# A one-core block kernel with attention, a recurrence and routed experts: router one-hots, bias table and last adds moved to other places in the order

## The chip, the core and the metric

The kernel runs on one core of one Trainium2 chip. The metric is the device time of one execution in microseconds (us). A core has five engines with queues of their own: TensorE (PE, whose weight loads are shown as PEld), VectorE (DVE), ScalarE (ACT), GpSimd (POOL) and SyncE (SP, which here only issues transfers). Each works through its instructions in the order in which they were put into its queue.

## What is computed

A sequence of 512 tokens with 1024 features goes through one block:

```python
proj = x @ w_in
o_a = dilated band attention of 3 groups x 4 heads, with a learned bias per distance bucket
o_b = a gated recurrence of 8 heads (forget gate f, running sums of log f)
o_c = attention of 4 heads over a memory of 256 rows
merged = sum of gate_i * (o_i @ w_branch_i)
x = layer_norm(ALPHA * x + merged @ w_out)                    # ln1
eid, weights = two experts of the best of 4 groups, for each token
y = sum over a token's two experts of weight * ((silu(x @ w_gate) * (x @ w_up)) @ w_down)
x = layer_norm(ALPHA * x + y)                                 # ln2
```

All of it is float32. There are 32 experts, and their weights (100 MB) are read once.

## The kernel before, in words

The tokens stand in four tiles of 128 rows, called c = 0 to 3. A float32 product of the first part is made of three matmuls of rounded parts (high by high, high by low, low by high); `split` (L82 to L84) makes the parts, the high one by a cast on ACT (L83), the low one by a subtraction on DVE (L84). The order of the instructions on each engine is made by a scheduler from the program's order and the dependences; it may pull an instruction ahead of others if its operands and its buffers are free. Inside `tc.manual_schedule(engines=...)` the named engines keep the order of the source.

**Start** (L148 to L166). Ten matmuls of a zeroed tile on itself run while the first rows are loaded. Then eight pieces of x arrive, each is split, and the first product `acc0` (a forget gate of the recurrence) is accumulated piece by piece.

**Forget gates** (L241 to L268). `forget(hd)` makes a product, a Sigmoid on ACT and a linear map on DVE for each of eight heads. `log_sums(hd)` takes the Ln on ACT and a running sum on DVE. Sigmoid and Ln need different activation tables, so that table loads stand between them (L244, L249).

**Memory attention** (L271 to L307), in the pool `c`, and then two gates `sgc` of it, whose tiles have the tag `sg` in the pool `gate` (three buffers).

**Bias table** (L311 to L334), in a pool `a0` of its own, opened when `c` is closed. The table of 32 buckets by 12 heads is loaded and split (L313 to L320); then for five pieces of 512 columns (the last has 256) GpSimd loads the bucket one-hots into `bk` (L327), ACT casts them into `bkr` (L329), PE multiplies (L331), ACT copies the result into `rows` (L333), and GpSimd stores them into DRAM, `bias_d` (L334). `bias_copies(h)` (L336 to L339) later spreads them over rows of `rep_d`, with three transfers per head.

**Recurrence** (L343 to L499), in a pool `b` that is opened after `a0` is closed. GpSimd clears `batt` and `bq` (L485, L487), `hgrn_front` makes the products of a head and copies one of them into `bw` on ACT (L352), and `hgrn_back` does the rest.

**Band attention, merge and first norm.** `residual` (L757) adds x and takes statistics; `norm_and_route(c)` (L707) normalises tile c, transposes it, multiplies by the router's weights, finds the two experts of each token on DVE (L721 to L734), counts the tokens of each expert before this one with PE (L739), and lets `picked(c, 0, oh0)` (L700, L743) make the one-hots of the first pair of experts: for each row of a pair's 128 slots the token that it takes. `gain_and_store(c)` (L745) multiplies by the gain and adds the offset, on GpSimd for tiles 0 to 2 and on DVE for tile 3, and stores the rows for the later gathers.

**Experts** (L1084 on). The 32 experts are treated as 16 pairs. `gather(p)` (L803) brings a pair's tokens: for p = 0 and 1 (`PEG = 2`) PE multiplies the four tiles of x1 with one-hots (L814, 8 matmuls per tile, each seen as two records); the one-hots of pair 1 are made by `picked` inside `gather(1)` (L811), on DVE. Later pairs are fetched from DRAM by an indirect transfer (L799). `gate_up(p)` (L829) multiplies by the first two weight matrices, `down` (L1048) by the third. The weights come through a ring of 33 buffers of 512 KB (`ring`, L658), in the order of use, issued by SP; a buffer is loaded again when the matmuls of its expert are done with it. In the loop p = 0 makes `gate_up(0)`, `tables` and `overflow_tables` (the slots, tokens and weights of all pairs, mostly small DVE instructions) and then `gather(1)`.

**End** (L1172 to L1225). DVE and PE are in source order. Each of the four tiles gets x1, the outputs of pairs 0 to 13 read back from DRAM (`back[c]`, two parts that `both(c)`, L1180, adds up on DVE) and the outputs of the last two pairs, added up in PSUM by `begin` and `finish`; `norm_out` (L1139) takes statistics on DVE (L1143), scales and stores. Tiles 0 to 2 use ACT (L1158) and GpSimd (L1159) for the last steps, tile 3 DVE alone (L1156). `both(2)`, `both(3)` and the addition of `back[3]` to tile 3 of x1 (L1216 to L1220) stand on DVE between the norms of the tiles.

Of the kernel before, what the change touches and what calls it, by code (L numbers as in the profile page):

```python
# [10 lines left out]
F32 = mybir.dt.float32  # L11
# [21 lines left out]
PEG = 2  # L33
# [3 lines left out]
def build(tc, ins, out, dbg=None):  # L37
# [117 lines left out]
    with tc.tile_pool(name="xs", bufs=2, side="right") as xsp:  # L155
        for k in range(8):
# [8 lines left out]
            for n, (wt, m) in enumerate(((w0[0], xh), (w0[0], xl), (w0[1], xh))):  # L165
                TE.matmul(acc0, wt[:, ks], m[:, k, :], start=k == 0 and n == 0, stop=k == 7 and n == 2)  # L166

# [102 lines left out]

    och = T(op_, [128, 4, 512], F32R, tag="oh4")  # L271
# [37 lines left out]


    with tc.tile_pool(name="a0", bufs=2, side="right") as tp:  # L311
        tab = T(tp, [97, 12], tag="tab")
        V.memset(tab, 0.0)  # L313
        for r0 in (0, 64):
            V.memset(tab[r0:r0 + 33, :], NEG)
            G.dma_start(tab[r0:r0 + 32, :], ins["rel_bias"])
        tabr, tabh = (T(tp, [97, 12], F32R, tag=t) for t in ("tabr", "tabh"))
        S.copy(tabr[0:64, :], tab[0:64, :])
        S.copy(tabh, tab)
        V.tensor_tensor(tabr[64:97, :], tab[64:97, :], tabh[64:97, :].bitcast(F32), op=OP.subtract)  # L320
        for j in range(5):
            w = min(512, 2304 - j * 512)
            js = slice(j * 512, j * 512 + w)
            bk = T(tp, [97, 512], tag="bk")
            V.memset(bk[32:64, :w], 0.0)
            for r0 in (0, 64):
                G.dma_start(bk[r0:r0 + 33, :w], ins["bucket"][:, js])  # L327
            bkr = T(tp, [97, 512], F32R, tag="bkr")
            S.copy(bkr[:, :w], bk[:, :w])  # L329
            pt = bank("sc")  # L330
            TE.matmul(pt[:12, :w], tabr, bkr[:, :w], start=True, stop=True)  # L331
            rows = T(tp, [12, 512], tag="rows")
            S.copy(rows[:, :w], pt[:12, :w])  # L333
            G.dma_start(bias_d[:, js], rows[:, :w])  # L334
# [361 lines left out]
    oh0 = T(lp, [128, 4, 128], tag="oh0")  # L696
# [3 lines left out]
    def picked(c, p, to):  # L700

        for e in range(2):
            m = 2 * p + e
            V.tensor_scalar(to[:, c, e * 64:(e + 1) * 64], i64, cums[:, c, m:m + 1], memb[:, c, m:m + 1],
                            op0=OP.is_equal, op1=OP.mult)

    def norm_and_route(c):  # L707

        r = x1[:, c, :]
        mu, sd = scales(lp, stats[:, c])  # L710
        xT = T(lnp, [128, 8, 128], tag="x1T")
# [614 lines left out]
```

## Time and profile before

| what | value |
|---|---|
| median of 3 runs | 1138.49 us (1136.7 to 1140.42) |
| the profiled execution, its own time | 1141.1 us |
| its span, first to last instruction | 1138.7 us |
| mean granted TensorE clock | 0.993 of full |
| busy: PE, DVE, ACT, POOL | 96%, 43%, 39%, 7% |
| bytes moved by DMA | 201 MB, 177 GB/s on average |

The span is the time between the first and the last instruction in the trace; the own time of the execution holds a little more, 2.4 us here. A row of a timeline gives start, duration, engine, line, operation and tiles, and in brackets how long the engine was idle before it and what ended that. Busy times of PE are of pipelined matmuls whose ends are modelled.

### The profile page before, as it was taken

How to read it: one execution, taken by the hardware profiler on the slowest of the kernel's cores; microseconds unless marked ns; L12 is line 12 of the kernel's file. 1: busy time of each engine (PE TensorE's matmuls, PEld its weight loads, DVE VectorE, ACT ScalarE, POOL GpSimd, SP SyncE). 2: the span in 40 equal slices, each digit the busy share in tenths (PEclk: the TensorE clock that was granted, in tenths of full speed). 3: DMA queues.
4: the chain of work that ended last, by engine and by line, in shares of the span. 5: the costliest groups of instructions: out<-in, count | busy, mean ns of one | idle time of the engine just before them, and what ended most of it. 6: DMA issues, size and time to landing. Idle time of an engine off the chain costs nothing.

```text
span 1138.7 us, 17136 instructions
## 1 busy us (share of the span) xinstructions
PE 1087.6 (96%) x6859; PEld 782.2 (69%) x6859; DVE 492.2 (43%) x985; ACT 446.4 (39%) x756; POOL 82.6 (7%) x107
## 2 busy tenths in 40 slices
PE   9999989999999999999999999999999999888884
PEld 6788778778888887887887887888776333332332
DVE  5554467777777323223223223336467111111126
ACT  7965556666666433233233233224114111111112
POOL 1000330000000000000000001000051211110003
PEclk9999999999999999999999999999999999999998
DMA  8742442222222432332331323633956999999992
GB/s 281 235 128 78 119 135 66 83 66 75 83 59 67 117 100 64 103 93 64 103 94 54 96 93 112 216 93 112 382 218 225 378 406 408 400 398 406 408 372 79
DMA packets 70482, 201.22 MB, mean 177 GB/s; under 512 B 16924, under 2 KB 19064, under 8 KB 70400
## 3 DMA queue, kind: packets, MB, share of 16 engines
q1 hardware_dynamic: 63216, 183.92, 46.1%
q0 software_dynamic: 7184, 16.17, 4.1%
q8 instruction: 55, 0.90, 0.3%
q14 instruction: 27, 0.22, 0.1%
HBM read 191.54 MB, written 17.81 MB: 184 GB/s over the span
## 4 chain that ended last, share of the span: by engine, by line
PE 80%; DMA 9%; ACT 6%; DVE 3%; issue 1%; POOL 0%; DVEq 0%; SPq 0%; ACTq 0%; POOLq 0%
PE pj L131 50%; PE pj L838 7%; DMA raw<-in_wexp_dram 7%; PE o L1054 4%; PE tr L222 3%; PE pj L765 2%; PE o L765 2%; ACT wh L83 1%; PE o L570 1%; PE sc L542 1%; PE sc L412 1%; ACT L244 1%; PE sc L548 1%; PE o L304 1%; ACT L249 1%
## 5 line engine op out<-in xcount | busy, mean ns | idle before, releaser
L84 DVE TENSOR_TENSOR wl<-raw,wh 128x1024 fp32r<-128x1024 f32 (+1 forms) x129 | 148.0, 1149 | 253.2 <-PE pj L131 188.3
L83 ACT CAST wh<-raw 128x1024 fp32r<-128x1024 f32 (+1 forms) x137 | 132.6, 969 | 234.5 <-PE pj L131 223.9
L131 PE MATMUL pj<-xh,wh 128*128 128x512 f32 x760 | 203.2, 401 | 3.7 <-ACT bw L352 3.5
L131 PE MATMUL pj<-xl,wh 128*128 128x512 f32 x760 | 196.6, 396 | 0.0
L131 PE MATMUL pj<-xh,wl 128*128 128x512 f32 x760 | 189.9, 392 | 0.0
L131 PEld LDWEIGHTS pj<-xh,wl 128*128 128x128 f32 x760 | 142.7, 188 | 31.1
L131 PEld LDWEIGHTS pj<-xh,wh 128*128 128x128 f32 x760 | 139.9, 189 | 33.4 <-ACT bw L352 3.9
L131 PEld LDWEIGHTS pj<-xl,wh 128*128 128x128 f32 x760 | 142.1, 189 | 29.6
L838 PE MATMUL pj<-raw,xs 128*64 128x512 f32 x432 | 118.5, 599 | 6.4 <-DMA raw<-in_wexp_dram 5.3
L838 PEld LDWEIGHTS pj<-raw,xs 128*64 128x64 f32 x432 | 35.1, 136 | 67.8 <-issue 46.0
L1054 PE MATMUL o<-raw,ehT 128*64 128x512 f32 x204 | 54.2, 617 | 1.2 <-ACT ehT L1064 0.5
L198 ACT ACTIVATE esg<-pj 128x256 f32<-128x256 f32 x16 | 6.2, 384 | 124.5 <-PE pj L838 124.5
L199 DVE SCALAR_TENSOR_TENSOR esg<-esg,pj 128x256 f32<-128x256 f32 x16 | 6.7, 420 | 107.3 <-ACT esg L198 107.3
L609 POOL DMA_DIRECT2D x<-in_xc_dram x4 | 2.1, 538 | 549.1 <-ACT oh L83 549.1
L1114 DVE TENSOR_SCALAR yp<-o,wsl 128x512 f32<-128x512 f32 x14 | 10.5, 750 | 65.5 <-PE o L1054 65.4
L1054 PEld LDWEIGHTS o<-raw,ehT 128*64 128x64 f32 x204 | 16.9, 140 | 28.2 <-issue 22.6
L131 PE MATMUL pj<-oh,wh 128*128 128x512 f32 x128 | 33.8, 393 | 1.4 <-issue 1.4
L131 PE MATMUL pj<-ol,wh 128*128 128x512 f32 x128 | 33.7, 393 | 0.0
L131 PE MATMUL pj<-oh,wl 128*128 128x512 f32 x128 | 33.3, 392 | 0.0
L214 DVE SCALAR_TENSOR_TENSOR sg<-sg,pj 128x512 f32<-128x512 f32 x16 | 11.0, 687 | 42.0 <-PE pj L131 42.0
L131 PEld LDWEIGHTS pj<-oh,wh 128*128 128x128 f32 x128 | 24.0, 188 | 6.5 <-issue 1.4
L131 PEld LDWEIGHTS pj<-oh,wl 128*128 128x128 f32 x128 | 24.0, 188 | 5.2
(399 smaller groups left out, 1460.8 us busy)
## 6 DMA issues: line engine op xcount, KB each, us to landing
raw<-in_wexp_dram SPq DMA_DIRECT2D x159, 512.0 KB, 10.8
raw<-in_w_in_dram SPq DMA_DIRECT2D x95, 512.0 KB, 3.6
wh<-in_wexp_dram SPq DMA_DIRECT2D x18, 512.0 KB, 11.0
wl<-in_wexp_dram SPq DMA_DIRECT2D x15, 512.0 KB, 12.2
yd<-merged SPq DMA_DIRECT2D x8, 512.0 KB, 7.0
raw<-in_w_kv_dram SPq DMA_DIRECT2D x8, 512.0 KB, 3.6
raw<-in_w_bb_dram SPq DMA_DIRECT2D x8, 512.0 KB, 3.6
raw<-in_w_out_dram SPq DMA_DIRECT2D x8, 512.0 KB, 3.7
```

Of the source, the lines that this page charges most:

```text
L83: S.copy(h, src)
L84: (eng or V).tensor_tensor(l, src, h.bitcast(F32), op=OP.subtract)
L131: TE.matmul(acc, wt[:, k * 128:(k + 1) * 128], m[:, k, :], start=n == 0, stop=n == 3 * kt - 1)
L222: TE.transpose(pt[:, j * 128:(j + 1) * 128], src[:, j * 128:(j + 1) * 128], ident)
L244: S.activation(nat(f), cls(acc), AF.Sigmoid)
L249: S.activation(f, f, AF.Ln, scale=oml[:, hd:hd + 1], bias=lb[:, hd:hd + 1])
L304: TE.matmul(o[:, cs], v[:, js], pT[:, js], start=j == 0, stop=j == 1)
L412: TE.matmul(sa4[g * 32:(g + 1) * 32, n, j], X[:, 2 + n, gs], X[:, 2 + n, gs], start=True, stop=True)
L542: TE.matmul(s1[g * 32:(g + 1) * 32, i * 256:(i + 1) * 256], qs[0][:, c * 128 + g * 32:c * 128 + (g + 1) * 32], ks[0][:, lows[g] * 128:lows ...
L765: TE.matmul(acc, m[:, k, cs], w[:, j * 512:(j + 1) * 512], start=k == 0 and n == 0, stop=k == 7 and n == 2)
L838: TE.matmul(acc[rows_, :], xs[:, j * 2 + k, rows_], raws[2 * p + q, j][:, k * 512:(k + 1) * 512], start=j == 0 and k == 0, stop=j == 3 and ...
L1054: TE.matmul(acc[rows_, :], hT[:, k * 128 + q * 64:k * 128 + (q + 1) * 64], raws[2 * p + q, 4 + k][:, n * 512:(n + 1) * 512], start=k == 0, ...
```

## The change

Five edits: (1) two small matmuls on a part of `xl` follow each of the first seven pieces of the first product. (2) The bias table moves from behind the memory attention to a place ahead of it, behind `log_sums`; its pool goes, its tiles are taken from the pools of constants, of gates (`sg`) and from `obl`. (3) `norm_and_route` makes the one-hots of both pairs at once; in `gather(1)` the matmuls of tiles 1 to 3 are queued behind the last matmul of `gate_up(0)`. (4) For tile 3 the DVE instructions keep the source's order, with the gain and offset placed among the router's steps, and every DVE instruction traced after it up to `gather(1)` is queued behind its last pick. (5) In the end, `both(2)`, `both(3)` and the addition to x1 go to GpSimd and stand behind `gate_up(15)`.

```diff
             for n, (wt, m) in enumerate(((w0[0], xh), (w0[0], xl), (w0[1], xh))):
                 TE.matmul(acc0, wt[:, ks], m[:, k, :], start=k == 0 and n == 0, stop=k == 7 and n == 2)
+            if k < 7:
+                x0 = xl[:, k, 0:128].bitcast(F32)
+                for j in range(2):
+                    TE.matmul(pt, x0, x0, start=True, stop=True)
...
     for hd in range(NF):
         log_sums(hd)
+    tab = T(cp, [97, 12], tag="tab")
+    V.memset(tab, 0.0)
+    for r0 in (0, 64):
+        V.memset(tab[r0:r0 + 33, :], NEG)
+        G.dma_start(tab[r0:r0 + 32, :], ins["rel_bias"])
+    tabr, tabh = (T(cp, [97, 12], F32R, tag=t) for t in ("tabr", "tabh"))
...
+    for j in range(5):
+        w = min(512, 2304 - j * 512)
+        js = slice(j * 512, j * 512 + w)
+        bk = T(gp, [128, 512], tag="sg")[:97]
+        V.memset(bk[32:64, :w], 0.0)
+        for r0 in (0, 64):
+            G.dma_start(bk[r0:r0 + 33, :w], ins["bucket"][:, js])
+        bkr = obl[:97, j, :]
+        S.copy(bkr[:, :w], bk[:, :w])
+        pt = bank("sc")
+        TE.matmul(pt[:12, :w], tabr, bkr[:, :w], start=True, stop=True)
+        rows = T(gp, [128, 512], tag="sg")[:12]
+        S.copy(rows[:, :w], pt[:12, :w])
+        G.dma_start(bias_d[:, js], rows[:, :w])
...
     sgc = [gate(2, cb) for cb in range(2)]
-    with tc.tile_pool(name="a0", bufs=2, side="right") as tp:
-        tab = T(tp, [97, 12], tag="tab")
...
-    oh0 = T(lp, [128, 4, 128], tag="oh0")
+    ohp = [T(lp, [128, 4, 128], tag=f"oh{p}") for p in range(PEG)]
...
     for k in range(8):
             TE.matmul(acc, xT[:, k, :], wr[:, k, :], start=False, stop=k == 7)
+        if c == 3:
+            V.tensor_tensor(r[:, hs[0]], r[:, hs[0]], l1g[:, hs[0]], op=OP.mult)
+            V.tensor_tensor(r[:, hs[0]], r[:, hs[0]], l1b[:, hs[0]], op=OP.add)
         V.max(gm[:, c, :], acc[:, 0:8])
...
         S.copy(cums[:, c, :], cum)
-        picked(c, 0, oh0)
+        if c == 3:
+            V.tensor_tensor(r[:, hs[1]], r[:, hs[1]], l1g[:, hs[1]], op=OP.mult)
+        picked(c, 0, ohp[0])
+        if c == 3:
+            V.tensor_tensor(r[:, hs[1]], r[:, hs[1]], l1b[:, hs[1]], op=OP.add)
+        return picked(c, 1, ohp[1])
...
+        if c < 3:
+            residual(c, 1, acc)
+            norm_and_route(c)
+        else:
+            with tc.manual_schedule(engines={mybir.EngineType.DVE}):
+                residual(c, 1, acc)
+                routed = norm_and_route(c)
         gain_and_store(c)
+    behind = ExitStack()
+    behind.enter_context(tc.issue_after(routed.ins))
...
+        late = ExitStack()
         if p < PEG:
-            oh_ = oh0 if p == 0 else T(mp, [128, 4, 128], tag="ohg", bufs=1)
+            oh_ = ohp[p]
             pts = [bank("o" if p == 0 else "tr") for _ in range(2)]
             for c in range(4):
-                if p > 0:
-                    picked(c, p, oh_)
+                if p == 1 and c == 1:
+                    late.enter_context(tc.issue_after(gate_last[0].ins))
...
             xs = gather(p + 1)
+            if p == 0:
+                behind.close()
...
         def both(c):
-            V.tensor_tensor(back[c][0], back[c][0], back[c][1], op=OP.add)
+            (V if c < 2 else G).tensor_tensor(back[c][0], back[c][0], back[c][1], op=OP.add)
...
         gu = gate_up(15, xs, first)
+        both(2)
+        both(3)
+        G.tensor_tensor(x1[:, 3, :], x1[:, 3, :], back[3][0], op=OP.add)
         sg = hidden(gu)
...
         norm_out(accs[0], 0, False)
-        both(2)
         finish(1)
         norm_out(accs[1], 1, False)
-        both(3)
-        V.tensor_tensor(x1[:, 3, :], x1[:, 3, :], back[3][0], op=OP.add)
         finish(2)
```

## Rows read from the trace of the kernel before

**Rows 1.** The page's first part: the span, and busy time of the engines.

```profile
span 1138.7 us, 17136 instructions
PE 1087.6 (96%) x6859; PEld 782.2 (69%) x6859; DVE 492.2 (43%) x985; ACT 446.4 (39%) x756; POOL 82.6 (7%) x107
```

**Rows 2.** Busy time of each engine by stretch, with granted clock and DMA share.

```profile
core 0: us, PE busy (x) PEld busy (x) DVE busy (x) ACT busy (x) POOL busy (x), PEclk, DMA share, GB/s
5.60:15.20 9.60, 8.39 (x25) 4.17 (x24) 6.88 (x18) 6.04 (x11) 0.00 (x0) 1.00 1.00 370
15.20:60.40 45.20, 44.70 (x193) 35.80 (x193) 27.78 (x38) 44.14 (x50) 0.00 (x0) 1.00 0.71 234
...
66.00:127.00 61.00, 60.50 (x383) 51.66 (x382) 30.69 (x81) 33.57 (x78) 0.91 (x2) 1.00 0.33 103
...
145.60:149.20 3.60, 0.10 (x1) 0.00 (x0) 3.60 (x9) 2.50 (x4) 3.60 (x6) 1.00 0.04 11
149.20:154.60 5.40, 5.39 (x17) 4.27 (x18) 4.53 (x13) 1.93 (x2) 3.73 (x8) 0.68 0.96 255
...
870.00:1100.00 230.00, 208.78 (x929) 79.27 (x925) 43.13 (x104) 34.03 (x64) 30.02 (x31) 0.99 1.01 398
...
1112.70:1130.80 18.10, 9.90 (x31) 5.20 (x29) 17.61 (x29) 5.18 (x10) 8.74 (x6) 0.96 0.22 82
```

**Rows 3.** Timeline from the last store of the bias table to the recurrence's next product.

```profile
141.10 0.50 POOL L334 DMA_DIRECT2D biasd<-rows  x1 [0.55 <-ACT rows L333]
...
145.04 0.53 POOL L485 MEMSET batt<- 128x512 f32 x1 [0.87 <-DMA biasd<-rows]
...
148.08 1.07 ACT L352 COPY bw<-pj 128x512 f32<-128x512 f32 x1
...
149.21 3.29 PE L131 MATMUL pj<-xh,wh 128*128 128x512 f32 x8 [3.51 <-ACT bw L352]
```

**Rows 4.** Groups of ACT instructions in 125 to 145.6 us: those of the bias table.

```profile
L329 ACT CAST bkr<-bk 97x512 fp32r<-97x512 f32 (+1 forms) x5 | 2.9, 573 | 1.0 <-DMA bk<-in_bucket_dram 1.0
L333 ACT COPY rows<-sc 12x512 f32<-12x512 f32 (+1 forms) x5 | 2.6, 530 | 0.7 <-PE sc L331 0.4 <-DMA biasd<-rows 0.2
```

**Rows 5.** Transfers issued in 0 to 62 us: KB each, median us to landing.

```profile
wr<-in_wr_dram POOLq DMA_DIRECT2D x1, 384.0 KB, 7.2
```

**Rows 6.** Tile 3's last steps: DVE's picks by line, then PE's timeline.

```profile
L704 DVE TENSOR_SCALAR ohg<-kc,cums,memb x8: 298/309/314, 856.6 to 863.5; 128x64 f32<-128x64 f32 x8
...
859.20 0.53 DVE L704 TENSOR_SCALAR oh<-kc,cums,memb 128x64 f32<-128x64 f32 x2
...
859.79 2.05 PE L814 MATMUL o<-oh,x 128*128 128x128 f32 x16
861.68 0.83 PE L814 MATMUL tr<-ohg,x 128*128 128x128 f32 x6
862.44 7.09 PE L838 MATMUL pj<-raw,xs 128*64 128x512 f32 x32
```

**Rows 7.** The end: groups of DVE, one of POOL, transfers read back, and PE and DVE waits.

```profile
L1181 DVE TENSOR_TENSOR raw<-raw,raw 128x1024 f32<-128x1024 f32 x4 | 4.8, 1211 | 0.0
L1220 DVE TENSOR_TENSOR x<-x,raw 128x1024 f32<-128x1024 f32 x1 | 2.2, 2170 | 0.0
...
L749 POOL TENSOR_TENSOR x<-x,l1g x6: 1254/1271/1289, 824.4 to 844.0; 128x512 f32<-128x512 f32 x6
...
raw<-yd SPq DMA_DIRECT2D x8, 512.0 KB, 10.1
...
1100.15 1.59 SPq L1126 DMA_DIRECT2D raw<-yd  x2
...
1117.02 1.98 PE L1137 MATMUL pj<-raw,ident 128*128 128x512 f32 x4 [1.16 <-DVE raw L1181]
...
1123.31 1.98 PE L1137 MATMUL o<-x,ident 128*128 128x512 f32 x4 [2.47 <-DVE x L1220]
...
1126.13 1.28 DVE L1143 BATCH_NORM_STATS2 lnst<-o 128x6 f32<-128x512 f32 x2
```

More of the change, by code (lines that the diff above doesn't have):

```diff
@@ L268, in build @@
         log_sums(hd)
+    tab = T(cp, [97, 12], tag="tab")
[4 more added lines that the diff above has]
+    tabr, tabh = (T(cp, [97, 12], F32R, tag=t) for t in ("tabr", "tabh"))
+    S.copy(tabr[0:64, :], tab[0:64, :])
+    S.copy(tabh, tab)
+    V.tensor_tensor(tabr[64:97, :], tab[64:97, :], tabh[64:97, :].bitcast(F32), op=OP.subtract)
+    for j in range(5):
[12 more added lines that the diff above has]
+        G.dma_start(bias_d[:, js], rows[:, :w])
     och = T(op_, [128, 4, 512], F32R, tag="oh4")
@@ L307, in build @@
     sgc = [gate(2, cb) for cb in range(2)]
-    with tc.tile_pool(name="a0", bufs=2, side="right") as tp:
-        tab = T(tp, [97, 12], tag="tab")
[L313 to L334, printed above, removed]
     def bias_copies(h):
@@ L703, in picked @@
             m = 2 * p + e
-            V.tensor_scalar(to[:, c, e * 64:(e + 1) * 64], i64, cums[:, c, m:m + 1], memb[:, c, m:m + 1],
-                            op0=OP.is_equal, op1=OP.mult)
+            last = V.tensor_scalar(to[:, c, e * 64:(e + 1) * 64], i64, cums[:, c, m:m + 1], memb[:, c, m:m + 1],
+                                   op0=OP.is_equal, op1=OP.mult)
+        return last
     def norm_and_route(c):
@@ L710, in norm_and_route @@
         mu, sd = scales(lp, stats[:, c])
+        hs = [slice(j * 512, (j + 1) * 512) for j in range(2)]
         xT = T(lnp, [128, 8, 128], tag="x1T")
@@ L742, in norm_and_route @@
         S.copy(cums[:, c, :], cum)
-        picked(c, 0, oh0)
+        if c == 3:
[4 more added lines that the diff above has]
+        return picked(c, 1, ohp[1])
     def gain_and_store(c):
         r = x1[:, c, :]
-        for j in range(2):
+        for j in range(2 if c < 3 else 0):
             js = slice(j * 512, (j + 1) * 512)
-            (V if c == 3 else G).tensor_tensor(r[:, js], r[:, js], l1g[:, js], op=OP.mult)
-            (V if c == 3 else G).tensor_tensor(r[:, js], r[:, js], l1b[:, js], op=OP.add)
+            G.tensor_tensor(r[:, js], r[:, js], l1g[:, js], op=OP.mult)
+            G.tensor_tensor(r[:, js], r[:, js], l1b[:, js], op=OP.add)
         G.dma_start(x1d[c * 128:(c + 1) * 128, :], r)
@@ L784, in build @@
             out_rows(acc, c, k, w1[k])
-        residual(c, 1, acc)
-        norm_and_route(c)
+        if c < 3:
[5 more added lines that the diff above has]
+                routed = norm_and_route(c)
         gain_and_store(c)
     dump("x1", x1)
+    behind = ExitStack()
+    behind.enter_context(tc.issue_after(routed.ins))
     p1x.close()
@@ L817, in gather @@
             xg = xgs[p % AHEAD]
+        late.close()
         for j in range(2):
@@ L827, in gather @@
         return xs
+    gate_last = [None]
     def gate_up(p, xs, amid=None):
@@ L837, in gate_up @@
                     rows_ = slice(q * 64, (q + 1) * 64)
-                    TE.matmul(acc[rows_, :], xs[:, j * 2 + k, rows_], raws[2 * p + q, j][:, k * 512:(k + 1) * 512],
-                              start=j == 0 and k == 0, stop=j == 3 and k == 1)
+                    gate_last[0] = TE.matmul(acc[rows_, :], xs[:, j * 2 + k, rows_],
+                                             raws[2 * p + q, j][:, k * 512:(k + 1) * 512],
+                                             start=j == 0 and k == 0, stop=j == 3 and k == 1)
         return acc
```

## The prediction

> **What bounds the kernel now.** I read the page first: the span is 1138.7 us and PE is busy for 96% of it [rows 1]. With a PE that full, an edit is worth only what it takes out of PE's waits, or out of a stretch that something else sets. So I cut the span into stretches and looked for the engine that is full in each [rows 2]. Five things are to be seen. In 5.6 to 15.2 us the transfers are full (share 1.00), and PE already has its full clock. In 15.2 to 60.4 us, the forget gates, PE is full (44.70 of 45.20 us), but so is ACT (44.14): each of the two would hold up the other. In 66 to 127 us PE is full and ACT has 61.0 - 33.6 = 27.4 us to spare. From 145.6 to 149.2 us PE does next to nothing, and the clock granted in the 5.4 us behind it is 0.68, a mix of the two levels of 1.2 and 2.4 GHz. From 870 to 1100 us the transfers are full (1.01) while PE is not (208.8 of 230 us): the experts' weights set the pace. And in the last 18.1 us DVE is full (17.61) and PE half idle.
>
> The timeline around the gap at 146 us says what made it [rows 3]: the last store of the bias table is issued at 141.10, GpSimd clears a tile of the next pool only at 145.04, when that store has landed, ACT gets to the copy into `bw` at 148.08, and PE's next product starts at 149.21 after a wait of 3.51 us. The pool of the bias table is closed by its last store, and the recurrence's pool waits for it.
>
> **Part 1, the small matmuls at the start.** Fourteen of them, two records each, at 2.05/16 = 0.12 to 0.13 us per record of that shape [rows 6], are 3.4 to 3.6 us of PE work. The clock there is 1.00 already [rows 2], so nothing is won. What covers them is the arrival of x: the transfers are at share 1.00. If that cover were gone, PE's idle 9.60 - 8.39 = 1.2 us would take the first part and 2.4 us would be left. I take 0, nearer to the cover, with 0 to +2.4 as ends.
>
> **Part 2, the bias table.** Removed: the wait of 3.51 us [rows 3], and the slow clock behind it, 5.40 x (1 - 0.68) = 1.7 us [rows 2]: 5.2 us together. With the pool `a0` gone, the recurrence's pool has only the memory attention's to wait for, which is closed some 20 us before.
>
> What is late next depends on where the moved steps land. They are twelve loads and five stores on GpSimd's queue, some clears on DVE, ten casts and copies on ACT, and five products on PE. GpSimd and DVE have room [rows 2]. PE's five products move from one full stretch to another: 0. ACT's ten cost 2.9 + 2.6 = 5.5 us [rows 4]. All their buffers are free from the start, so the scheduler may pull them far ahead, as it does with another load on that queue, which is issued long before its place in the source and lands after 7.2 us [rows 5]. Bounds: 0 if they fall in the memory attention, where ACT has 27.4 us to spare; 5.5 us if all fall in 15.2 to 60.4 us, where ACT has 1.1 us and PE none. I take a point between: the loads come some 7 us after their issue, so about half of ACT's 3.6 idle us before 15.2 can be used, and the 1.1 us behind: 5.5 - 1.8 - 1.1 = 2.6 us of cost. Part 2 is then -2.6 us, from -5.2 to +0.3. The transfers that spread the table (L339) come earlier as well; they are what fills the 5.4 us at share 0.96 [rows 2], and go into stretches at 0.71 or 0.33, so I count nothing for them.
>
> **Parts 3 and 4, the one-hots and DVE's order at tile 3.** PE works without a pause from the last residual to `gate_up(0)` at 862.44 [rows 6]. Between, it does all 64 records of `gather(0)` and 20 of `gather(1)`, six of them in the 0.76 us before `gate_up(0)`. After the change at most the 16 of tile 0 can stand there: four records, 0.5 us, go behind for sure. DVE's picks for tile 3 stand at 859.20; five of the other pair's picks at 0.31 us stood between the steps of tile 3's search [rows 6]. Without them, and with the gain partly behind, I expect those picks about 1.0 us earlier. So `gate_up(0)` starts 0.5 us earlier if PE's fillers set it, up to 1.7 us (1.0 and the six records) if the picks did; I take 0.9. On the other side, DVE's tables can begin only after tile 3's picks; PE takes up their product only when `gate_up(0)` is over, 7 us later, which hides it. Each pair's weights are reloaded into buffers that `gate_up(0)` is the first to free, and from there on transfers are full until 1100 us [rows 2], so what `gate_up(0)` gains is kept to the end of the experts, whatever PE does between. The 48 records put behind it are hidden by the transfers.
>
> **Part 5, the end.** PE waits 1.16 us for `both(2)` and 2.47 us for the addition to x1 [rows 7]; without them the last tile's statistics start at 1126.13 - 3.63 = 1122.5. DVE allows it: 1.21 + 1.21 + 2.17 = 4.6 us of its 17.61 go away. GpSimd must be in time: the last part read back is issued at about 1101.4 and lands 10.1 us later, 1111.5; two additions of 1024 columns at 2 x 1.27 us each [rows 7] end at 1116.6, and PE needs the result at 1123.31 - 3.63 = 1119.7. That leaves 3.1 us. The row of the addition, 2.17 us against 1.21 for the same shape [rows 7], shows what DVE pays when GpSimd works on such rows too: 1 us. `both(1)` on DVE now may pay it, ahead of products that have about that much time. I take -3.4, between 0 and -3.63.
>
> The Trainium skill (SBUF — State Buffer, Who interferes with whom) says that a DVE instruction with two SBUF inputs and a GpSimd instruction that reads SBUF lock each other out for the whole instruction. By that rule `both(1)` could lose the 2.5 us of a GpSimd addition instead of 1 us, and the end would gain about 2 us less; the row speaks for 1 us, but only once.
>
> **The sum.** 0 - 2.6 - 0.9 - 3.4 = -6.9 us. The profiled execution took 1141.1 us, so 1134.2 by its own time; it stands 2.6 us above the median of the runs, 1138.49, against which the forecast is 1131.6 us.
>
> **Rivals.**
> - *The table's casts are hidden wholly.* They fall into the memory attention, or the gates' Ln steps give way. For it: ACT's 27.4 us there. Against: nothing holds the casts back until then. Part 2 is -5.2, the sum -9.5: 1129.0 us.
> - *The table's casts are paid in full*, in the stretch where ACT and PE are both full. Part 2 is +0.3, the sum -4.0: 1134.5 us. For it: 44.14 of 45.20 us.
> - *The two engines of the end get in each other's way.* `both(1)` and GpSimd's additions hold each other up, the additions pass their 3.1 us of room, and only the wait of 1.16 us is saved: the sum is 0 - 2.6 - 0.9 - 1.2 = -4.7, 1133.8 us. Against: the long wait of 2.47 us had a DVE instruction of 2.17 us in it, which goes in any case.
> - *The table holds up the start: slower.* ACT and PE work in order; a cast placed behind a bucket load that lands late keeps back the casts of x and of the weights behind it. Loads at that time take up to 7.2 us to land [rows 5], and there are five rounds of load, cast, product, copy and store through three shared buffers. At 3 us lost per round the loss is 15 us against gains of 9.5 us: 1138.5 + 5.5 = 1144 us. It decides from 9.5/5 = 1.9 us per round on. Against: the scheduler has other work to put in front, and DVE and GpSimd are not full.
>
> **How the numbers follow.** Chances: the forecast 0.38, casts hidden 0.23, casts paid in full 0.22, the end's contention 0.10, the start held up 0.07. A measurement of this kernel can tell 0.3%, 3.4 us, from no change, so faster means under 1135.1 us. Nearly all of the forecast and of the first rival lie under it, two thirds of the second and of the contention: 0.78. Slower is the last rival: 0.07. The rest is 0.15. The range goes from 2 us below the hidden casts, 1127.0, for the upper ends of parts 3 to 5, to 2 us above the casts paid in full, 1136.5, for part 1's; what is left out is the held-up start and the far ends.
>
> **What would show it.** Part 2: no wait of PE before the recurrence's third product and a clock of 1.00 behind it; the casts of the table found before 66 us, and PE's waits for ACT up by about 2.6 us there. Parts 3 and 4: from the end of the forget gates' stretch to `gate_up(0)`, tile 3's picks about 1 us earlier against the last residual, and transfers still full from there to the last weights. Part 5: the last tile's statistics about 3.4 us earlier against the end of the last weights, DVE's `both(1)` at 1.2 or at 2.2 us. It is wrong if PE waits for a bucket cast at the start, if the forget gates' stretch grows by over 6 us, or if PE still waits for the addition to x1.

## The result, and the profile after

The changed kernel takes 1149.37 us (median of 6 runs, 1147.65 to 1150.96) where the kernel before takes 1138.04 (6 runs): a ratio of 1.0098, 95% interval 1.0083 to 1.0114. It is 11 us slower; the forecast was 7 us faster. The profiled execution took 1149.06 us by its own time, with a mean granted clock of 0.994 (before: 0.993). The traced execution of the kernel before took 1141.1 us, 3 us over its median, so that the two traces differ by 8 us and not by 11.

The page's first part after the change, which answers to [rows 1]:

```profile
span 1146.8 us, 17185 instructions
PE 1095.9 (96%) x6887; PEld 788.2 (69%) x6887; DVE 488.9 (43%) x982; ACT 446.6 (39%) x756; POOL 89.7 (8%) x110
```

The span grew by 8.1 us and PE's busy time by 8.3, for 28 records of small matmuls more. PE is idle for as long as before (50.9 us, 51.1): the same work takes it longer. When things happen says where (starts from the timelines of the two traces, us):

| start of | before | after | later by |
|---|---|---|---|
| first product of a whole weight tile (L131) | 15.26 | 16.80 | 1.5 |
| the recurrence's own steps | 173.86 | 175.11 | 1.3 |
| the band attention | 434.82 | 443.13 | 8.3 |
| the 288 products before the first norm | 724.98 | 737.03 | 12.1 |
| `gate_up(0)` | 862.44 | 876.80 | 14.4 |
| the last tile's statistics | 1126.13 | 1134.18 | 8.1 |

So most of the time is lost between 174 and 737 us, some at the start and up to `gate_up(0)`, and some is won behind that. From 174 to 737 us the change edits nothing. The groups of PE's commonest instructions show what happened there, first of the kernel before, then of the changed one (busy us, mean ns of one, idle before):

```profile
L131 PE MATMUL pj<-xh,wh 128*128 128x512 f32 x760 | 203.2, 401 | 3.7 <-ACT bw L352 3.5 <-ACT wh L83 0.2
...
L131 PE MATMUL pj<-xh,wl 128*128 128x512 f32 x760 | 189.9, 392 | 0.0
```

```profile
L131 PE MATMUL pj<-xh,wh 128*128 128x512 f32 x760 | 205.0, 402 | 0.3 <-ACT wh L83 0.3
...
L131 PE MATMUL pj<-xh,wl 128*128 128x512 f32 x760 | 192.5, 395 | 0.0
```

The same 760 matmuls, of the same shape, at a granted clock of 1.00 in both, take 3 ns more each where nothing else is in the way (last rows). Matmuls overlap, so the pace from start to start is the better measure. The chain of waits has one piece without any pause, the 288 products (start, duration), before and after:

```profile
724.98 66.15 PE pj L131 x288
```

```profile
737.03 67.40 PE pj L131 x288
```

That is 1.25 us on 288, 4.3 ns each. From start to start within groups of eight, such products took 228.9 ns before and some 232 to 235 after, in every stretch from 15 us on. The kernel makes some 2,660 of them with 512 columns: 9 to 12 us.

The stretches of [rows 2], after the change (the last one shifted by 10 us):

```profile
5.60:16.80 11.20, 10.37 (x54) 8.12 (x53) 6.40 (x18) 6.05 (x11) 1.58 (x3) 1.00 1.02 332
16.80:60.40 43.60, 43.34 (x186) 34.59 (x186) 26.65 (x37) 42.90 (x49) 0.00 (x0) 1.00 0.71 241
60.40:66.00 5.60, 4.43 (x29) 3.83 (x27) 3.24 (x4) 5.56 (x7) 1.55 (x3) 1.00 0.23 79
66.00:127.00 61.00, 57.19 (x365) 49.21 (x365) 30.45 (x71) 34.48 (x77) 10.86 (x21) 1.00 0.47 140
145.60:149.20 3.60, 3.60 (x17) 2.94 (x16) 2.66 (x4) 1.15 (x2) 0.00 (x0) 1.00 0.22 18
149.20:154.60 5.40, 5.40 (x24) 4.36 (x24) 3.57 (x8) 2.53 (x3) 0.00 (x0) 1.00 0.30 99
880.00:1110.00 230.00, 209.13 (x957) 78.92 (x951) 43.82 (x108) 34.41 (x65) 30.25 (x31) 1.00 1.01 397
```

The gap at 146 us is gone and the clock behind it is 1.00. PE now idles in the memory attention instead: 3.8 of 61 us from 66 to 127, where it idled 0.5 before [rows 2]. The table's steps there, of PE and then of ACT:

```profile
66.97 0.41 PE L294 MATMUL sc<-ol,tabr 97*12 97x512 f32 x1 [2.13 <-ACT ol L292]
74.21 0.41 PE L294 MATMUL sc<-ol,tabr 97*12 97x512 f32 x1 [1.25 <-ACT ol L292]
...
84.20 0.29 PE L294 MATMUL sc<-ol,tabr 97*12 97x256 f32 x1 [0.73 <-ACT ol L292]
...
73.54 0.62 ACT L292 CAST ol<-sg 97x512 fp32r<-97x512 f32 x1 [1.32 <-DMA sg<-in_bucket_dram]
...
83.74 0.40 ACT L292 CAST ol<-sg 97x256 fp32r<-97x256 f32 x1 [1.90 <-DMA sg<-in_bucket_dram]
```

PE waits for ACT's cast at three of the five rounds. At the last two of these ACT itself waits for the bucket load: loads and row stores share three buffers `sg` and one queue, so a load waits until an earlier round's store has landed. At the first and longest, 2.13 us, it does not: that cast runs at 66.30 without a pause before it, behind the last steps of the forget gates, and ACT is busy for 5.56 of the 5.60 us up to 66. And the end, which answers to [rows 7] (DVE's second `both`, GpSimd's additions, the last statistics):

```profile
1121.35 1.22 DVE L1209 TENSOR_TENSOR raw<-raw,raw 128x1024 f32<-128x1024 f32 x1
...
1121.51 3.27 POOL L1209 TENSOR_TENSOR raw<-raw,raw 128x1024 f32<-128x1024 f32 x1 [33.66 <-DMA raw<-yd]
1125.19 2.36 POOL L1209 TENSOR_TENSOR raw<-raw,raw 128x1024 f32<-128x1024 f32 x1 [0.40 <-PE sc L1064]
...
1134.18 1.30 DVE L1171 BATCH_NORM_STATS2 lnst<-o 128x6 f32<-128x512 f32 x2
```

Both waits of PE in [rows 7] are gone. The last statistics start 19.4 us behind the last product of `gate_up`, against 23.9 before.

### The profile page after: what moved, and what is told of

It is laid out like the page before. It is cut to its first block, busy times and chain, and to the rows that moved or that the text cites. A ratio compares the mean times of both kernels' runs of the same rounds, so it can differ in the third digit from the quotient of the medians.

```text
span 1146.8 us, 17185 instructions
## 1 busy us (share of the span) xinstructions
PE 1095.9 (96%) x6887; PEld 788.2 (69%) x6887; DVE 488.9 (43%) x982; ACT 446.6 (39%) x756; POOL 89.7 (8%) x110
## 4 chain that ended last, share of the span: by engine, by line
PE 76%; DMA 12%; issue 7%; DVE 2%; ACT 2%; POOL 0%; DVEq 0%; ACTq 0%; POOLq 0%; SPq 0%
PE pj L131 50%; DMA raw<-in_wexp_dram 11%; PE pj L863 5%; PE tr L226 3%; PE o L1080 3%; PE pj L779 2%; PE o L779 2%; PE o L573 1%; PE sc L545 1%; PE sc L415 1%; PE sc L551 1%; PE o L333 1%; PE sc L726 1%; PE o L581 1%; PE o L454 1%
## 5 line engine op out<-in xcount | busy, mean ns | idle before, releaser
L131 PE MATMUL pj<-xh,wh 128*128 128x512 f32 x760 | 205.0, 402 | 0.3 <-ACT wh L83 0.3
L131 PE MATMUL pj<-xl,wh 128*128 128x512 f32 x760 | 197.7, 397 | 0.0
L131 PE MATMUL pj<-xh,wl 128*128 128x512 f32 x760 | 192.5, 395 | 0.0
L131 PEld LDWEIGHTS pj<-xh,wl 128*128 128x128 f32 x760 | 142.9, 188 | 33.5
L131 PEld LDWEIGHTS pj<-xl,wh 128*128 128x128 f32 x760 | 142.0, 188 | 31.9
L131 PEld LDWEIGHTS pj<-xh,wh 128*128 128x128 f32 x760 | 139.7, 189 | 30.9 <-ACT wh L83 1.4
L1080 PE MATMUL o<-raw,ehT 128*64 128x512 f32 x204 | 51.5, 599 | 1.3 <-ACT ehT L1090 0.5
L131 PE MATMUL pj<-oh,wh 128*128 128x512 f32 x128 | 35.4, 406 | 0.0
L131 PE MATMUL pj<-ol,wh 128*128 128x512 f32 x128 | 34.4, 398 | 0.0
L131 PE MATMUL pj<-oh,wl 128*128 128x512 f32 x128 | 33.8, 395 | 0.0
L131 PEld LDWEIGHTS pj<-oh,wh 128*128 128x128 f32 x128 | 24.4, 192 | 5.5
L131 PEld LDWEIGHTS pj<-oh,wl 128*128 128x128 f32 x128 | 24.1, 188 | 5.8
```

What stands on the lines that cost most here:

```text
L131: TE.matmul(acc, wt[:, k * 128:(k + 1) * 128], m[:, k, :], start=n == 0, stop=n == 3 * kt - 1)
L1080: TE.matmul(acc[rows_, :], hT[:, k * 128 + q * 64:k * 128 + (q + 1) * 64], raws[2 * p + q, 4 + k][:, n * 512:(n + 1) * 512], start=k == 0, ...
```

## The experiments

**Theory A.** The three small tiles of the bias table lay in a pool of their own on the right-hand side of SBUF. The change puts them into the constants' pool, which lies ahead of the pool `wp` of the weights. In the compiled programs each takes 64 bytes of a partition, so that `wh` starts at 33888 instead of 33696, while the operand streamed through it, `xh`, stays at 193504. The theory is that this move alone sets the pace. Theory B: the loss is in waits, and the pace comes from something else.

### The move of 192 bytes alone, and taken back

```diff
+    V.memset(T(cp, [128, 48], tag="pad"), 0.0)
     wp = es.enter_context(tc.tile_pool(name="wp", bufs=3))
```

> The kernel before with one unused tile of 192 bytes laid ahead of the weight pool and nothing else changed (one memset of it on DVE). The trace after the change shows the 512-column products of pool wp at 232.4 to 233.7 ns from start to start where they took 228.9 before, and the three small table tiles push that pool 192 bytes up. Theory A (the place of the weights in SBUF sets the pace): the same slow pace appears, some 2,660 products times 3.5 to 4.7 ns = 9.3 to 12.5 us, so 1147.4 to 1150.6 us. Theory B (the table's waits and loads are the loss, the pace comes from something else in the changed program): 1138 us, 228.9 ns.

Measured: 1146.9 us, ratio 1.0061 (1.0039 to 1.0083), a little under the range of theory A. The 288 products of its chain (line numbers are one higher):

```profile
731.73 67.39 PE pj L132 x288
```

An unused tile gives the changed kernel's pace and 7 us of its 11. Theory B falls. Two kernels take the move back in the changed kernel:

```diff
-    tab = T(cp, [97, 12], tag="tab")
+    tab = T(tp, [97, 12], tag="tab", bufs=1)
...
-    tabr, tabh = (T(cp, [97, 12], F32R, tag=t) for t in ("tabr", "tabh"))
+    tabr, tabh = (T(tp, [97, 12], F32R, tag=t, bufs=1) for t in ("tabr", "tabh"))
+    V.memset(T(tp, [128, 80], tag="pad", bufs=1), 0.0)
```

> The changed kernel with its three small table tiles, and a pad that fills them up to 512 bytes, in the short-lived pool c on the right-hand side, so that the weight pool lies where it lay before the change; all else as changed. Theory A: the pace goes back to 228.9 ns and 9.3 to 12.5 us with it: 1137 to 1140 us. Theory B: the pace stays, 1149 us.

Measured: 1144.34 us, 1.0046 (1.0029 to 1.0063), with the 288 products at 66.14 us again. The pace came back, but not all of the expected time, because this placement has a mishap of its own: ACT stood 3.08 us at 23 us before a cast of the table, and PE, at 30 us, 2.71 us for the weights queued behind.

```profile
23.25 0.20 ACT L282 CAST tabr<-tab 64x12 fp32r<-64x12 f32 x1 [3.08 <-DMA tab<-in_rel_bias_dram]
```

So the second one leaves the table where the change has it and adds 64 bytes to its 192:

```diff
+    V.memset(T(cp, [128, 16], tag="pad"), 0.0)
     wp = es.enter_context(tc.tile_pool(name="wp", bufs=3))
```

> The changed kernel as it is, with an unused tile of 64 bytes laid ahead of the weight pool, so that the pool lies 256 bytes above its place before the change instead of 192. If the place counts modulo 256 bytes: 228.9 ns a product again, and the 7 to 9 us of theory A come back, 1140 to 1142 us; if it counts modulo 512, or if only the exact place of before is fast, 232.4 ns or another pace, 1146 to 1150 us. The rest of the loss, which the run with the table on the right showed (5.7 us over before at the old pace), is looked for in the waits of this trace.

Measured: 1140.74 us, 1.0022 (1.0007 to 1.0038).

```profile
730.11 66.14 PE pj L132 x288
```

The changed kernel with 64 unused bytes more is at the old pace and 8.7 us faster (1.0098 - 1.0022 = 0.0076 of 1138). This is the size of the term that the forecast left out, measured in the changed kernel itself. 256 bytes from the old place are as good as the old place.

### Which distance

The next four have the later parts of the change alone (see below), with 96 or 64 unused bytes ahead of `wp`, or, in the last, 64 bytes behind `xl`, which move `xh` and everything on the right-hand side instead of the weights.

```diff
+    V.memset(T(cp, [128, 24], tag="pad"), 0.0)
     wp = es.enter_context(tc.tile_pool(name="wp", bufs=3))
```

> The kernel with the later parts alone (one-hots, order of DVE, GpSimd's additions), with 96 unused bytes ahead of the weight pool: its tiles then start at a multiple of 512 bytes. If a start at a multiple of 512 is the fast place and before only a near one, the pace falls below 228.9 ns and the time below 1136 (at 225 ns by 10 us); if before's place is already at the floor: 228.9 ns, 1136 us; if it is a bad place: 232.4 ns or more, 1144 us.

> The same with 64 bytes: the weights start at 480 modulo 512, as the first operand xh does. One look for the pace: 228.9 ns if only half of the places are bad (modulo 128, say: 96 bad, 32 good), 232.4 ns if 96 modulo 128 is the bad place, since 480 is 96 modulo 128.

> The kernel of the run before once more, timed: the later parts alone and the weights at 480 modulo 512, where xh lies. One look gave 1128.5 us and 226.9 ns a product, 2 ns under before. If that pace is the place's: some 2,660 products times 2 ns = 5.3 us, with the later parts' 2.4 us 1138.3 - 7.7 = 1130.6 us (1128 to 1132). If the one look was a lucky execution: 1136 us as with the weights in their old place.

```diff
     xl = T(xp, [128, 8, 512], F32R, tag="xl")
+    V.memset(T(xp, [128, 16], tag="pad"), 0.0)
```

> The later parts alone, with the weights where they were (416 modulo 512) and the operand streamed through them moved instead: 64 unused bytes behind xl bring xh and xl from 480 to 416, and all of the right-hand side with them. The paces so far, by the distance of xh from wh modulo 256: 0 gives 226.9 ns, 64 gives 228.9, 128 gives 232.4, 224 gives 233.4. If the distance counts: 226.9 ns and about 1130 us. If the place of the weights alone counts: 228.9 ns and 1136 us.

Measured: 96 bytes ahead of the weights 1142.98 us, 1.0042 (1.0026 to 1.0058); 64 bytes 1128.53 in a single execution and 1128.17 over six, 0.9917 (0.9896 to 0.9937); 64 bytes behind `xl` 1131.64, 0.9940 (0.9924 to 0.9955). The 288 products of the three, in this order:

```profile
733.97 67.39 PE pj L132 x288
```

```profile
720.99 65.50 PE pj L132 x288
```

```profile
721.93 65.50 PE pj L132 x288
```

| kernel | `wh` at | `xh` at | distance modulo 256 | 288 products, us |
|---|---|---|---|---|
| weights +64, or `xh` -64 | 33760, 33696 | 193504, 193440 | 0 | 65.50 |
| before | 33696 | 193504 | 64 | 66.15 |
| changed, +64 | 33952 | 193504 | 64 (320) | 66.14 |
| changed; before +192 | 33888 | 193504 | 128 | 67.40, 67.39 |
| weights +96 | 33792 | 193504 | 224 | 67.39 |

The expectation for 64 bytes by place modulo 128 missed: 480 is 96 modulo 128, as the changed kernel's place is, and was the fastest. That both ways to distance 0 give the same 65.50 us says that it is the distance that counts, not the place of the weights. Both ways also shift everything else on one side of SBUF against the other; that it is the pair of weights and streamed operand is the plain reading, which no run isolates. Five distances were run. They fit a rule modulo 256, for which the likeness of 64 and 320 is the only direct sign; what in the chip makes it was not found.

### The bias table alone

The kernel before with the block moved as the change moves it, its small tiles in pool `c` as above.

```diff
     for hd in range(NF):
         log_sums(hd)
+    tab = T(tp, [97, 12], tag="tab", bufs=1)
...
-    with tc.tile_pool(name="a0", bufs=2, side="right") as tp:
...
```

> The kernel before with the bias table's block moved as the change moves it and nothing else of the change, its small tiles in pool c as in the run before, so that the weights don't move. My forecast for this part was -2.6 us (-5.2 to +0.3), so 1135.4. Theory A, with what the trace after shows (the 3.5 us wait at 146 us and the slow clock behind it gone, -5.2; waits of 4.9 us in the memory attention for the table's casts and copies, and 1.5 us at the start): 1138 to 1140 us, no gain. Theory B: most of the loss is here, 1144 to 1149 us.

Measured: 1139.4 us, 1.0009 (0.9997 to 1.0022): no gain. Its waits of PE (total, times, longest, us):

```profile
PE sc L290 <- ACT ol L288: 3.9, 2, 2.6
...
PE pj L166 <- ACT xh L83: 1.7, 2, 1.4
```

The gap and the slow clock are gone (149.2 to 154.6 us at 1.00), 5.2 us; 3.9 us came back as waits for the casts and 1.3 us at the start, where the pieces of x arrive later beside the loads that now run there (6.9 us to landing at the median, 6.0 before; first full product at 16.58 instead of 15.26). One trace alone would not show the 1.3 us: in the twelve traces of kernels whose start is as before it stands at 14.80 to 16.87. But in all four with the table moved it stands at 16.53 to 16.80. In the trace of the table alone the granted clock fell behind PE's longest wait at either place too, here from 7.8 and from 66 us on:

```profile
7.80:12.00 4.20, 3.93 (x9) 2.67 (x9) 2.77 (x4) 2.45 (x4) 0.00 (x0) 0.59 1.03 335
...
66.00:70.00 4.00, 3.17 (x15) 3.08 (x15) 3.03 (x4) 2.48 (x5) 1.03 (x2) 0.57 0.53 194
```

The second costs 4.0 x 0.43 = 1.7 us more. The three traces that have the small matmuls of part 1 as well show 1.00 at both places, with first full products no earlier (16.53 to 16.80).

### The small matmuls alone

Two a round, as in the change; then one, and four (`range(1)`, `range(4)`).

```diff
                 TE.matmul(acc0, wt[:, ks], m[:, k, :], start=k == 0 and n == 0, stop=k == 7 and n == 2)
+            if k < 7:
+                x0 = xl[:, k, 0:128].bitcast(F32)
+                for j in range(2):
+                    TE.matmul(pt, x0, x0, start=True, stop=True)
```

> The kernel before with the 14 small products of the start alone. My forecast was 0 (0 to +2.4). With the table on the right the whole change stood 5.7 us over before, the table's move alone 0.9 over it and the later parts alone 2.4 below it: 7.2 us are left for the small products and for what the parts do together. That trace showed 1.3 us at the first full product, 2.7 us of a wait for the table's load on ACT, and 4 waits of PE for nothing but its own instruction stream (5.3 us together against 2.6 in before). Theory C (the small products pay at the start and shift the instruction stream): 1.3 to 4 us, 1140 to 1142.6 us, with more or longer waits of that kind between 220 and 375 us. Theory D (they are hidden, the rest is the table's wait): 1138.6 us.

> The kernel before with one small product a round instead of two, 7 in all. With 14 the run showed four waits of PE for its own instruction stream between 220 and 375 us, 5.4 us together; kernels without them show one or two, 1.1 to 2.8 us; the time rose 3.2 us. Theory C1 (the products push the stream behind them, and where its pieces end among the dense small products of that stretch decides): the waits lie elsewhere, fewer or shorter than with 14, and the time is 1138.5 to 1140 us. Theory C2 (any extra products cost in proportion): half of 3.2 us, 1139.9 us, with the same four waits. Theory D (nothing to do with them): as before in both.

> The kernel before with four small products a round, 28 in all. Seven cost 1.7 us and showed waits of PE for nothing but its stream of 3.2 us in all, fourteen 3.3 us and 5.4 us; before has 2.6. Theory C1 (where they push the stream): the waits lie at other places again and need not be longer than with 14; the start takes 2 to 3 us more than with 14, since each pair took some 0.36 us on PE: 1141 to 1145 us. Theory C2 (in proportion): 6.6 us over before, 1144.6 us, with waits of some 10 us.

Measured: with 14 of them 1141.6 us, 1.0028 (1.0011 to 1.0045); with 7, 1139.74, 1.0014 (1.0005 to 1.0023); with 28, 1141.44, 1.0031 (1.0016 to 1.0047). They are not free, and their price is not in proportion: C2 falls. The first full product starts at 15.64 with 14, at 16.23 with 7 and at 18.33 with 28; beside the 14.80 to 16.87 of unedited starts only the last stands clear. The rest is in the recurrence, where PE waits for nothing that the views show. Those waits, of the kernel before, with 14, with 7, and with 28:

```profile
PE pj L131 <- issue: 1.4, 1, 1.4
...
PE sc L412 <- issue: 1.2, 1, 1.2
```

```profile
PE sc L420 <- issue: 2.6, 2, 1.7
PE sc L423 <- issue: 1.8, 1, 1.8
...
PE sc L416 <- issue: 1.0, 1, 1.0
```

```profile
PE sc L420 <- issue: 1.8, 1, 1.8
PE sc L423 <- issue: 1.1, 1, 1.1
```

```profile
PE sc L423 <- issue: 1.7, 1, 1.7
PE pj L131 <- issue: 1.6, 1, 1.6
```

They stand at other instructions each time, most of them among the recurrence's matmuls of 32 and 64 columns (L412 to L423), and come to 2.6, 5.4, 3.2 (with one of 0.3 that is not shown) and 3.3 us. That is no chance of one execution: thirteen traces of kernels without small matmuls show one or two such waits, 0.5 to 3.0 us in all, and the four with 14 of them the same four waits at the same matmuls, 5.1 to 6.1 us. A long one can also cost clock. The stretch from 260 to 300 us, before and with 14:

```profile
260.00:300.00 40.00, 40.00 (x383) 32.47 (x382) 30.31 (x69) 27.93 (x53) 0.00 (x0) 1.00 0.24 73
```

```profile
260.00:300.00 40.00, 38.24 (x350) 31.68 (x349) 27.28 (x62) 24.57 (x50) 0.00 (x0) 0.96 0.19 60
```

A wait of 1.76 us, and a granted clock of 0.96 over the 40 us, which is another 40 x 0.04 = 1.6 us. (A wait of 1.72 us at 227 us in the same trace cost none: 220 to 260 us is at 1.00.) The traced executions with 14 and with 28 took 1146.1 us each, 4.5 us or more over their medians, so they show more than a usual execution loses.

What PE waits for stands in the same traces, among the transfers: one queue carries instructions in packets of 16 KB, 55 of them in each run, as many as PE's 13,850 or so records need at some 250 to a packet. With 14, around the wait of 1.76 us (the packet that moves from 285.0 to 286.3 us, and PE's rows):

```profile
q8 instruction: 1, 0.02, 5.5%
...
285.67 0.27 PE L423 MATMUL sc<-bx 128*64 128x64 f32 x1
287.71 0.62 PE L423 MATMUL sc<-bx 128*64 128x64 f32 x7 [1.76 <-issue]
```

The packet ends at 286.20, and PE goes on 1.5 us later. So it is each time: the 42 such waits between 174 and 442 us in all 19 traces end 1.2 to 1.6 us behind the end of one of these packets, and each began after that packet had started. PE waits there for its own instructions, as far as a trace can show it. That bears out C1: instructions put in ahead move the places where one packet ends and the next is needed, and what counts is which matmuls stand there. The Trainium skill (Runtime: NRT & Kernel Launch, Instruction fetch mechanics) says that an engine's instructions are fetched in blocks of 16 KiB and that crossing a block is mostly hidden. The traces agree: of the 20 packets of that stretch, before and with 14, two and four go with a wait.

### The later parts

The end alone, the one-hots with DVE's written order alone, and both:

```diff
-            V.tensor_tensor(back[c][0], back[c][0], back[c][1], op=OP.add)
+            (V if c < 2 else G).tensor_tensor(back[c][0], back[c][0], back[c][1], op=OP.add)
...
         gu = gate_up(15, xs, first)
+        both(2)
+        both(3)
+        G.tensor_tensor(x1[:, 3, :], x1[:, 3, :], back[3][0], op=OP.add)
```

> The kernel before with GpSimd's additions at the end alone. My forecast for them was -3.4 us (0 to -3.6). The run with all later parts was 2.4 us faster than before; its trace has the first expert's product 1.1 us later than before, the last weights' product at the same time, and 4.5 us less behind it. Theory: the whole gain is here, 1134 to 1136 us. Rival (the one-hots' part has a share of the gain): 1137 us or more.

> The kernel before with the early one-hots, the picks queued behind the first product and DVE's written order in the last tile, and nothing else. My forecast was -0.9 us. The traces of the runs with all later parts show the first expert's product waiting 1.7 us for ACT's copy of its gathered rows, a wait that 6 picks of the second pair filled before, and starting 1.1 us later; the weights' last product was no later for it. Theory E (the wait took the place of the gain): 0 to +1.7 us, 1138 to 1139.7 us, the first product at 863.5. Rival (forecast): 1137.1 us, the first product by 862.0.

> The kernel before with the later parts of the change alone: both one-hots made early, the picks queued behind the first product, DVE's written order in the last tile, and the additions of tiles 2 and 3 on GpSimd at the end; the start and the table as before, so the weights don't move. My forecast for these parts was -0.9 and -3.4, 1133.8 us. The trace after gained 4 us behind its last memory product (12 us late at 737, 8 us late at the end). Theory A: 1134 us (1133 to 1135). Theory B, if the later parts change the pace: 1138 us or more.

Measured: the end 1133.88 us, 0.9965 (0.9950 to 0.9981); the one-hots 1140.66, 1.0018 (1.0002 to 1.0035), 1 us above theory E's range; both 1136.24, 0.9974 (0.9959 to 0.9989), between theories A and B. The end is worth its forecast and a little more; the one-hots lose. PE around `gate_up(0)`, and ACT there, in the kernel with the one-hots alone:

```profile
858.89 1.95 PE L834 MATMUL o<-oh,x 128*128 128x128 f32 x16
...
863.24 3.22 PE L861 MATMUL pj<-raw,xs 128*64 128x512 f32 x14 [1.73 <-ACT xs L847]
```

```profile
859.49 3.23 ACT L1070 ACTIVATE xg<-kc 128x512 f32<-128x512 f32 x6 [1.43 <-DVE x L754]
862.63 0.56 ACT L847 COPY xs<-o 128x512 f32<-128x512 f32 x1
```

`gather(0)` ends at 858.89 + 1.95 = 860.84, a microsecond earlier than before, 859.79 + 2.05 = 861.84 [rows 6]. (The 861.51 of the next expectation is the end of PE's part of `gather(1)`.) But ACT's copy of its result stands behind six clears of `xg`, the buffers of the later gathers, which lie where tile 3's work was and wait for DVE's last addition to it. Before the change ACT ran them from 856.73 on, in its idle time:

```profile
856.73 1.15 ACT L1046 ACTIVATE xg<-kc 128x512 f32<-128x512 f32 x2 [3.34 <-DVE gi L723]
...
861.53 0.57 ACT L826 COPY xs<-o 128x512 f32<-128x512 f32 x1
```

DVE's written order puts that addition behind tile 3's search and picks, and the clears with it. To show it, the clears were put on GpSimd:

```diff
-            S.mul(xgs[j][:, h * 512:(h + 1) * 512], i512, 0.0)
+            G.memset(xgs[j][:, h * 512:(h + 1) * 512], 0.0)
```

> The one-hots' part alone once more, with the six clears of xg as memsets on GpSimd instead of ACT. With ACT's clears they start at 859.49, behind DVE's last addition to tile 3, take 3.23 us, and ACT's copy of the gathered rows stands behind them at 862.63, though the gather ended at 861.51; before the change they ran from 856.73 on. Theory F (the clears hold the copy back): the copy starts at about 861.5, the first expert's product at 862.1 instead of 863.24, without its wait of 1.73 us, and 1 us or so less in all: 1139.5 us. Rival (the gather itself or DVE's copy is the limit): the product stays at 863.2 and the time at 1140.7 us.

Measured: 1137.38 us, 1.0003 (0.9992 to 1.0014).

```profile
861.21 5.37 PE L861 MATMUL pj<-raw,xs 128*64 128x512 f32 x24
```

No wait, and `gate_up(0)` starts 2.0 us earlier than with ACT's clears, so theory F holds for the wait. The median's loss is no longer to be seen, but neither is a gain, and the intervals of the two runs overlap (1.0002 to 1.0035, 0.9992 to 1.0014).

### The fastest version

The kernel before with the end's additions on GpSimd and 64 unused bytes ahead of `wp`, and the one with the one-hots and GpSimd's clears as well:

> The kernel before with GpSimd's additions at the end alone and 64 unused bytes ahead of the weight pool, so that the weights lie at the distance 0 modulo 256 from the operand streamed through them: 226.9 ns a product. From the end alone (-4.1) and the pace (2,660 times 2 ns, -5.3): 1128.6 us. If the one-hots' part costs what the difference of the runs says (2.4), it beats the version with all later parts (1128.2) by as much: 1126 us.

> All later parts, the clears on GpSimd, and the weights at the distance 0. With ACT's clears it took 1128.2 us, the version without the one-hots' part 1125.7. Theory F: 1127 us, and 1125 at best if the whole cost of the one-hots' part was the clears. Rival: 1128.2 us.

Measured: 1125.66 us, 0.9881 (0.9861 to 0.9901), and 1127.37, 0.9905 (0.9889 to 0.9922). The first is the fastest version of the study, 1.2% under the kernel before and 2.2% under the changed one (0.9881 / 1.0098 = 0.978). The intervals of the two overlap a little; the one-hots add nothing that can be seen.

## Why the prediction was wrong

The forecast's sum was -6.9 us. The runs of the parts give, of 1138 us:

| part | forecast (ends) | measured (interval) |
|---|---|---|
| 1, small matmuls | 0 (0 to +2.4) | +3.2 (+1.3 to +5.1) |
| 2, bias table | -2.6 (-5.2 to +0.3) | +1.0 (-0.3 to +2.5) |
| 3 and 4, one-hots and DVE's order | -0.9 (-1.7 to -0.5) | +2.0 (+0.2 to +4.0) |
| 5, the end | -3.4 (-3.6 to 0) | -4.0 (-5.7 to -2.2) |
| pace of the products | not in the sum | +8.7 |

The first four make +2.2, and the changed kernel at the old pace stands at 1.0022, +2.5 us: the parts add up. With the pace, taken from the changed kernel with and without 64 unused bytes, it is +10.9, and 11.2 was measured. The kernel before with the 192 bytes alone gives 6.9 us (4.4 to 9.4) for the pace, which agrees.

**The step that failed** is in part 2: "PE's five products move from one full stretch to another: 0." The part was costed as instructions and loads, and its three small tiles as nothing. They move from a temporary pool to the constants, and every product of the 2,660 then runs at another pace, 228.9 ns from start to start before and some 232 to 235 after: 8.7 us in a term that was put at 0. The diff shows the move of the tiles; no row of the trace of before showed a price for it, so it should have stood in the sum as an unknown with two ends. No rival named it either: that the time went up was outside of all cases but one, and that one for another reason.

**Part 2, the rest.** The gap and the slow clock went, as forecast, 5.2 us. What was late next was weighed at the wrong place. ACT's casts did not lengthen the forget gates: ACT is busy 42.90 of 43.60 us there, PE 43.34. All but the first fell behind them into the memory attention, and PE stood 4.1 us there. About half, the wait of 2.13 us, is the rival "paid in full" a little later: ACT was still full when the cast came up. The other half, 1.25 and 0.73 us, fell where ACT had time to spare, which by the first rival would hide it. But an idle engine hides nothing when it stands in order before a load: the rounds go through three shared buffers, ACT waited 1.32 and 1.90 us for their loads, and PE, in order too, for ACT. That is the mechanism of the rival "the table holds up the start", at another place and at 0.4 us a round instead of 3, below the 1.9 us from which it decides.

**Part 1.** The cover was right and not enough. What the start pays is not clear of the spread of the traces; the loss comes 200 us later, from waits for PE's own instructions (5.4 us in all, 2.6 before), which sit at other places when instructions are put in ahead. The upper end of 2.4 us was an account of the start alone.

**Parts 3 and 4.** PE's side was right: the gather's part ahead of `gate_up(0)` gets shorter, and with the clears out of the way `gate_up(0)` starts 1.3 us earlier against the end of the products of L131 (70.0 us behind it, 71.3 before), where 0.9 was forecast. Tile 3's picks gave less of it than expected: against the last residual they come 0.4 us earlier (9.7 us behind its start, 10.1 before), not 1.0. Whether such a gain lasts to the end of the experts, as was forecast, is not shown: from the first to the last product of `gate_up` the 19 traces take 235.4 to 240.1 us. The step left out a queue that the moved step holds up: DVE's last addition to tile 3 frees the space that ACT clears, and ACT's copy is queued behind the clears.

**Part 5.** Right in sign, mechanism and place; 3.4 was forecast, 4.0 measured, and the trace has 4.5 us less between the last weights and the last statistics. The contention fell on the other engine: `both(1)` on DVE takes 1.22 us beside GpSimd, as without it, and GpSimd's addition beside it 3.27 us against 2.36 for the next, 0.9 us that nobody waits for. By the rule of the Trainium skill (SBUF — State Buffer, Who interferes with whom) the two lock each other out for a whole instruction. The trace agrees, with the cost on the one that came second: GpSimd's began 0.16 us behind DVE's. In the trace of before it was the other way round:

```profile
1120.76 3.62 POOL L1159 TENSOR_TENSOR raw<-raw,raw 128x512 f32<-128x512 f32 x2 [1.44 <-ACT raw L1158]
```

DVE's addition to x1 began at 1121.08, behind GpSimd's, and took 2.17 us [rows 7]. The 1 us that the forecast read from that row is the price of coming second, not of working beside GpSimd.

## What to carry to other kernels

A tile added to a pool moves all that lies behind it, and the pace of every matmul of this kernel hung on the distance between weights and streamed operand: when unedited work changes pace at the same clock, compare where the tiles lie, and try some unused bytes before anything else. When a step is moved, list what its last write lets go (a buffer, a pool) and what stands behind that on its engine's queue. And extra instructions on a full engine cost not only where they are put: they move the places where the engine has to wait for its next instructions.

## What the runs showed that was not expected

- Products of 512 columns with float32 parts go at 226.9 ns from start to start with `xh` at the distance 0 modulo 256 bytes from the weights, 228.9 at 64, some 232 to 235 at 128 and 233.4 at 224, at a granted clock of 1.00.
- PE stands 0.3 to 1.8 us at a time, mostly among matmuls of 32 and 64 columns, until 1.2 to 1.6 us after a 16 KB packet of instructions has moved (42 waits in 19 traces). The places shift with what is ahead of them in its stream, and the granted clock over the 40 us around one of the longest was 0.96.
- With the table's loads at the start and without the small matmuls, PE waited 1.39 us for x, and the granted clock of the next 4 us was 0.59; with the small matmuls it was 1.00 in three traces.
- GpSimd's addition of 1024 columns takes 0.9 us more when it begins inside a DVE addition of the same shape, which takes no longer for it.
